# Feed-forward groups of 4, 6, 6, 6 units instead of 6, 4, 6, 6 in a macaron encoder layer on one core

## Chip, core and metric

One NeuronCore of a Trainium2 chip runs the whole kernel. The metric is the device time of one execution in microseconds, as the median of several runs of the kernel before and of the changed one on the same chip.

## What is computed

One layer of a streaming encoder for 576 tokens (512 of a prompt, 64 of a sample), width 1024, all in float32:

```
x = x + 0.5 * rmsnorm(swiglu_1(rmsnorm(x)))
x = x + rmsnorm(concat(retention, diff_attention)(rmsnorm(x) @ w_in) @ w_out)
x = x + 0.5 * rmsnorm(swiglu_2(rmsnorm(x)))
swiglu(h) = (silu(h @ wg) * (h @ wu)) @ wd        # 1024 -> 2816 -> 1024
```

The change touches the two feed-forward networks alone. It alters no value that is computed, only the order in which the hidden units are worked through.

## The kernel before

**Data.** Activations lie transposed (width on the 128 partitions, tokens along the free axis). The tokens are cut into two halves of 256 and 320 (`HN`) for the plain products, and into a front and a back of 288 (`HT`) for the seven-product ones. Every float32 operand is split into a rounded part `hi` and a rest `lo`, and each product is made as three matmuls, hi*hi, hi*lo and lo*hi. For weights `Weights.part` (L99) does this: a DMA on the SP queue brings 256 KB into a `raw` buffer (three of them, five more `raw2` for the seven-product blocks), ScalarE casts it to `whi` (L125), VectorE subtracts to get `wlo` (L126). Twelve such pairs can be held. `run` (L441) converts the weights six parts ahead of the chunk that it is about to issue.

**Feed-forward.** The hidden width 2816 is 22 units of 128. Units 0 to 3 (`PLAIN`) are made by plain gate/up chunks: `gate_up` (L604) multiplies for one token half (48 matmuls, L418 to L420), scales by the row's 1/rms (L612), applies silu on ScalarE (L613), multiplies (L614), and splits the result into an `a` tile (L185 on ScalarE, L186 on VectorE). Units 4 to 21 are made by `fast_unit` (L499), a seven-product scheme for a 2x2 block product: seven products P1 to P7 of 12 matmuls each (L513 to L515, 288 columns) in place of eight, with sums of weight blocks (`wsum`, L114 to L119) and sums of activation blocks (`tb`). Units are collected in groups (`GROUPS`); after a group its part of the down projection runs as four output chunks j for each token half (`down`, L627; the matmuls are L418 to L420 again, reading `a`). The first group's down chunks are copied from PSUM to `y` by ScalarE (L640), those of later groups are added to `y` by VectorE (L642).

**What has to happen before the first seven-product matmul.** The activations that the scheme reads must carry the 1/rms, which the plain chunks do without. `renorm` (L457) therefore scales the eight x rows (`scale`, L469), makes four sums and splits them into `tb` (`sums`, L480 with L185 and L186), and splits x again into `hhi` and `hlo` (`again`, L185 and L186). It is a generator of 18 steps; `ffn` hooks it behind the items of the order: it starts behind item 3, and items 3 to 7 (the last plain ones) advance it. The x tiles are read by it to its end; the `y` tiles of the down projection then take over the buffers of x (both are `big` tiles), and x is loaded again later (`reload_x`).

**Order.** A group's plain chunks come first, in the order c0, c1, c2 of half 0, the same of half 1, then c3 of half 0 and c3 of half 1 (`halves`, L428). In the kernel before, the first group has the four plain units and two seven-product ones, so its seven-product matmuls follow the last plain chunk at once. Each engine works through its own queue in the order given; the order on each engine is laid down by the tile scheduler when the program is built. PSUM is held in two double-bank tiles `pm` and four single banks (`pa`, `pb`, `A` and others); chunks take them in turn (`product`, L399). The seven products of a unit use a `pm` tile named `CB` and a bank `A`.

Of the kernel before, what the change touches and what calls it, by code (L numbers as in the profile page):

```python
# [23 lines left out]
HN = (256, 320)  # L24
DFF = 2816
MT = DFF // P
GROUPS = (6, 4, 6, 6)
PLAIN = 4
RENORM_STEPS = 4
HT = T // 2  # L30
BIG, IN_FFN = 16, 4
EPS = 1e-6
# [8 lines left out]
FIRST, LAST_FFN, LAST_MIX = 3, 4, 3  # L41
# [107 lines left out]
class Layer:  # L149
# [417 lines left out]
    def ffn_weights(self, f):  # L567

        io, w = self.io, self.w
        plan, m = [], 0  # L570
        for gi, nk in enumerate(GROUPS):
            units = list(range(m, m + nk))
# [8 lines left out]
    def ffn(self, f, h, pre_g, post_g, next_g):  # L581
# [4 lines left out]
        after, act, ys = [], {}, []  # L586
        first = [sum(GROUPS[:gi]) for gi in range(len(GROUPS))]
        with tc.tile_pool(name=f"ffn{f}", bufs=1) as fp:
# [12 lines left out]
            def a_tile():  # L601
                return fp.tile([P, 2, T], F32R, tag="a", name="a", bufs=max(GROUPS))

# [23 lines left out]
            def down(gi, j, parts_):  # L627
                def fn(half):
                    final = next_g is None and gi == len(GROUPS) - 1
                    s = slice(HOFF[half], HOFF[half] + HN[half])  # L630
                    parts = self.product(parts_, half, lambda kt: [act[first[gi] + kt][:, p, s] for p in range(2)], True,
                                         final and j == 3)
                    if gi == 0 and len(ys) == j:
                        ys.append(self.big("y"))
                    if gi == 0:
                        y[half][j] = self.cut(ys[j], half)
                    t = y[half][j]
                    for c, ps in parts:
                        if gi == 0:
                            nc.scalar.copy(t[:, c, :], ps)  # L640
                        else:
                            nc.vector.tensor_tensor(t[:, c, :], t[:, c, :], ps, ALU.add)  # L642
                    if gi == len(GROUPS) - 1:
                        self.sublayer_out(y, acc, half, j, post_g)
                        if j == 3 and final and half == 0:
                            self.finish_natural(y[0], acc[0], xn)
                        elif j == 3:
                            self.start_boundary(half, y, acc, next_g, after)
# [13 lines left out]
            n_plain = len(order)  # L662
            for kind, what, parts in plan:
                if kind == "plain":
                    continue
                if kind == "down":
                    later.append((parts, down(*what, parts)))
                    if what[1] == 3:
                        final = what[0] == len(GROUPS) - 1
                        order += self.halves(later, 4 if final else 1, 4 if final else 0, final and next_g is None)  # L670
# [7 lines left out]
            def step_renorm(n):  # L678
                for _ in range(n):
                    if renorm:  # L680
                        try:
                            next(renorm[0])
                        except StopIteration:
                            renorm.pop()
# [6 lines left out]
            def at(i, fn):  # L691
                old = hook.get(i)
                hook[i] = (lambda: (old(), fn())) if old else fn
            at(FIRST, start_renorm)
            for i in range(FIRST, n_plain - 1):
                at(i, lambda: step_renorm(RENORM_STEPS))
            at(n_plain - 2, lambda: step_renorm(1))
            at(n_plain - 1, lambda: step_renorm(1))
            last = max(i for i, o in enumerate(order) if o[2] is None)
            at(last, lambda: self.reload_x(self.spill if f else self.io["x"]))  # L700
            if next_g is None:
# [641 lines left out]
```

## Time and profile before

| | |
|---|---|
| median of 3 runs | 1173.41 us (1172.97 to 1173.81) |
| the profiled execution, its own time | 1175.34 us |
| its span in the trace | 1173.6 us |
| TensorE busy | 1137.6 us, 97% |
| VectorE busy | 830.9 us, 71% |
| ScalarE busy | 571.4 us, 49% |
| mean granted TensorE clock | 0.987 of full |

Busy time of TensorE is modelled from start to end of pipelined matmuls, so 97% does not say that it ran at its full pace. Where it waited or ran slowly is read from start times: the time between the first matmul of a stretch and the first of the next, against another stretch with the same matmuls.

### The profile page before, as it was taken

Reading aid. Unit: us, or ns where it says so; the run is one execution under the profiler, and the core shown is the slowest. Engines: PE = TensorE matmul, PEld = TensorE weight load, DVE = VectorE, ACT = ScalarE, POOL = GpSimd, SP = SyncE. Lnnn points to the kernel's source line nnn. Section 1 sums busy time; section 2 is a strip of 40 time slices with the busy share of each in tenths; the row PEclk is TensorE's granted clock in tenths of the full one; section 3 lists DMA queues with packets and bytes.
Section 4 is the critical chain, followed back from the end, with each engine's and each line's share of the span. In section 5 each row is a group of like instructions: output and inputs, shape, how many; then the busy total and the mean of one; then the engine's idle time right before and its main releaser. Section 6 shows DMA issues by size and latency. Waiting matters only on the chain.

```text
span 1173.6 us, 21248 instructions
## 1 busy us (share of the span) xinstructions
PE 1137.6 (97%) x8322; PEld 1114.4 (95%) x8322; DVE 830.9 (71%) x1634; ACT 571.4 (49%) x1102; POOL 43.6 (4%) x84
## 2 busy tenths in 40 slices
PE   8989999999999999999999999996999999999997
PEld 8989999999999999899999999996999999999997
DVE  7985586876586599869574574899547778658735
ACT  7664452552354564455432455665435346325543
POOL 0000000000000031020001010000000000000000
PEclk9989999999999999999999999998999999999998
DMA  7133241342235133242222222421414223313402
GB/s 259 46 92 102 64 136 45 100 130 68 64 90 197 55 94 119 67 125 82 66 83 61 72 85 74 139 68 47 134 54 118 72 83 110 107 50 96 164 25 81
DMA packets 57315, 109.20 MB, mean 93 GB/s; under 512 B 7008, under 2 KB 10336, under 8 KB 57216
## 3 DMA queue, kind: packets, MB, share of 16 engines
q1 hardware_dynamic: 51856, 91.97, 26.7%
q0 software_dynamic: 4352, 14.68, 3.7%
q8 instruction: 65, 1.06, 0.4%
q10 hardware_dynamic: 1008, 1.20, 0.3%
q14 instruction: 34, 0.28, 0.1%
HBM read 100.23 MB, written 7.60 MB: 92 GB/s over the span
## 4 chain that ended last, share of the span: by engine, by line
PE 82%; DVE 9%; DMA 4%; ACT 3%; issue 1%; SPq 0%; DVEq 0%; ACTq 0%
PE pm L418 9%; PE pm L419 9%; PE pm L420 9%; PE A L513 6%; PE A L514 6%; PE A L515 6%; PE CB L513 5%; PE CB L515 4%; PE CB L514 4%; PE pb L418 2%; PE pa L418 2%; PE pb L420 2%; PE pa L419 2%; PE pa L420 2%; PE pb L419 2%; DVE wlo L126 2%
## 5 line engine op out<-in xcount | busy, mean ns | idle before, releaser
L125 ACT CAST whi<-raw 128x512 fp32r<-128x512 f32 x336 | 206.4, 619 | 242.0 <-PE pm L419 84.5
L126 DVE TENSOR_TENSOR wlo<-raw,whi 128x512 fp32r<-128x512 f32 x336 | 229.4, 688 | 113.6 <-ACT whi L125 109.3
L418 PE MATMUL pm<-hhi,whi 128*128 128x320 f32 (+1 forms) x496 | 152.0, 307 | 1.2 <-ACT hhi L253 1.2
L420 PE MATMUL pm<-hhi,wlo 128*128 128x320 f32 (+1 forms) x496 | 147.9, 299 | 0.4 <-DVE wlo L126 0.2
L419 PE MATMUL pm<-hlo,whi 128*128 128x320 f32 (+1 forms) x496 | 147.7, 298 | 0.3 <-DVE hlo L254 0.3
L420 PE MATMUL pm<-a,wlo 128*128 128x320 f32 (+1 forms) x448 | 133.0, 297 | 0.0
L419 PE MATMUL pm<-a,whi 128*128 128x320 f32 (+1 forms) x448 | 133.0, 297 | 0.0
L418 PE MATMUL pm<-a,whi 128*128 128x320 f32 (+1 forms) x448 | 132.7, 296 | 0.0
L513 PE MATMUL A<-tb,whi 128*128 128x288 f32 x432 | 129.7, 300 | 0.0
L514 PE MATMUL A<-tb,whi 128*128 128x288 f32 x432 | 128.5, 297 | 0.0
L515 PE MATMUL A<-tb,wlo 128*128 128x288 f32 x432 | 127.9, 296 | 0.0
L125 ACT CAST whi<-wsum 128x512 fp32r<-128x512 f32 x108 | 67.0, 621 | 84.3 <-PE pm L419 28.2
L513 PE MATMUL CB<-hhi,whi 128*128 128x288 f32 x288 | 86.6, 301 | 15.7 <-ACT e L529 8.8
L126 DVE TENSOR_TENSOR wlo<-wsum,whi 128x512 fp32r<-128x512 f32 x108 | 74.5, 690 | 34.5 <-ACT whi L125 33.0
L418 PEld LDWEIGHTS pm<-hhi,whi 128*128 128x128 f32 x496 | 94.1, 190 | 2.2 <-ACT hhi L253 1.5
L419 PEld LDWEIGHTS pm<-hlo,whi 128*128 128x128 f32 x496 | 94.1, 190 | 1.1 <-DVE hlo L254 0.5
L420 PEld LDWEIGHTS pm<-hhi,wlo 128*128 128x128 f32 x496 | 93.9, 189 | 1.0 <-DVE wlo L126 0.8
L515 PE MATMUL CB<-hhi,wlo 128*128 128x288 f32 x288 | 85.8, 298 | 0.0
L514 PE MATMUL CB<-hlo,whi 128*128 128x288 f32 x288 | 85.6, 297 | 0.0
L419 PEld LDWEIGHTS pm<-a,whi 128*128 128x128 f32 x448 | 85.0, 190 | 0.3 <-DVE a L186 0.3
L420 PEld LDWEIGHTS pm<-a,wlo 128*128 128x128 f32 x448 | 85.0, 190 | 0.0
L418 PEld LDWEIGHTS pm<-a,whi 128*128 128x128 f32 x448 | 84.9, 190 | 0.0
(333 smaller groups left out, 2926.2 us busy)
## 6 DMA issues: line engine op xcount, KB each, us to landing
raw<-in_w0gs SPq DMA_DIRECT2D x72, 256.0 KB, 2.7
raw<-in_w1gs SPq DMA_DIRECT2D x72, 256.0 KB, 2.7
raw<-in_win SPq DMA_DIRECT2D x56, 256.0 KB, 3.1
raw<-in_w0d SPq DMA_DIRECT2D x44, 256.0 KB, 2.7
raw<-in_w1d SPq DMA_DIRECT2D x44, 256.0 KB, 2.8
raw<-in_w0gu SPq DMA_DIRECT2D x16, 256.0 KB, 5.8
raw<-in_wout SPq DMA_DIRECT2D x16, 256.0 KB, 2.9
raw<-in_w1gu SPq DMA_DIRECT2D x16, 256.0 KB, 3.3
```

What stands on the lines that cost most here:

```text
L125: nc.scalar.copy(hi, raw)
L126: nc.vector.tensor_tensor(lo, raw, hi.bitcast(F32), ALU.subtract)
L418: nc.tensor.matmul(outs[c], lhsT=hi[:, k, cs], rhs=rh, start=kt == 0, stop=False)
L419: nc.tensor.matmul(outs[c], lhsT=hi[:, k, cs], rhs=rl, start=False, stop=False)
L420: nc.tensor.matmul(outs[c], lhsT=lo[:, k, cs], rhs=rh, start=False, stop=kt == len(kts) - 1)
L513: nc.tensor.matmul(out, lhsT=hi[:, k, :], rhs=rh, start=first and k == 0, stop=False, skip_group_check=True)
L514: nc.tensor.matmul(out, lhsT=hi[:, k, :], rhs=rl, start=False, stop=False, skip_group_check=True)
L515: nc.tensor.matmul(out, lhsT=lo[:, k, :], rhs=rh, start=False, stop=last and k == 3, skip_group_check=True)
```

## The change

`GROUPS` becomes (4, 6, 6, 6). The first group is then the four plain units alone. Its eight down half chunks (24 matmuls each, L418 to L420) stand between the last plain gate/up chunk and the first seven-product matmul; the 18 seven-product units follow as three groups of six. The number of matmuls, of weight parts and of down chunks is the same. `renorm` is advanced by three steps behind each of items 3 to 7 and is finished behind item 7 (before: four steps, then single ones, ended behind item 7 as well).

```diff
-GROUPS = (6, 4, 6, 6)
+GROUPS = (4, 6, 6, 6)
-RENORM_STEPS = 4
+RENORM_STEPS = 3
...
-            for i in range(FIRST, n_plain - 1):
+            for i in range(FIRST, n_plain):
                 at(i, lambda: step_renorm(RENORM_STEPS))
-            at(n_plain - 2, lambda: step_renorm(1))
-            at(n_plain - 1, lambda: step_renorm(1))
+            at(n_plain - 1, lambda: step_renorm(100))
```

TensorE, second feed-forward, end of the plain chunks: before (numbers behind a name are the scheduler's tile numbers).

```order
L418 MATMUL pm_9418<-hhi_8764,whi_8989 128x320
L419 MATMUL pm_9418<-hlo_8765,whi_8989 128x320
L420 MATMUL pm_9418<-hhi_8764,wlo_8990 128x320
L513 MATMUL CB_9490<-tb_9164,whi_9001 128x288
L514 MATMUL CB_9490<-tb_9165,whi_9001 128x288
L515 MATMUL CB_9490<-tb_9164,wlo_9002 128x288
```

The same place now:

```order
L418 MATMUL pm_9389<-hhi_8764,whi_8989 128x320
L419 MATMUL pm_9389<-hlo_8765,whi_8989 128x320
L420 MATMUL pm_9389<-hhi_8764,wlo_8990 128x320
L418 MATMUL pm_9488<-a_8898,whi_8995 128x256
L419 MATMUL pm_9488<-a_8898,whi_8995 128x256
L420 MATMUL pm_9488<-a_8898,wlo_8996 128x256
```

What follows the last plain chunk reads the `a` tiles of the plain units and no longer the `tb` of `renorm`.

VectorE, second feed-forward, around L612 of the last plain chunk (unit 3, half 1): before.

```order
L480 TENSOR_TENSOR sums_9172<-x3_4456,sums_9172 128x576
L186 TENSOR_TENSOR tb_9171<-sums_9172,tb_9170 128x576
L186 TENSOR_TENSOR hlo_8571<-x0_4453,hhi_8570 128x2x256
L186 TENSOR_TENSOR tb_9171<-sums_9172,tb_9170 128x576
L186 TENSOR_TENSOR hlo_8637<-x1_4454,hhi_8636 128x2x256
L186 TENSOR_TENSOR hlo_8701<-x2_4455,hhi_8700 128x2x256
L186 TENSOR_TENSOR hlo_8765<-x3_4456,hhi_8764 128x2x256
L612 TENSOR_TENSOR gu_9467<-pm_9418,r_pre_9150 128x640
L186 TENSOR_TENSOR hlo_8571<-x0_4453,hhi_8570 128x2x32
```

The same place now:

```order
L186 TENSOR_TENSOR tb_9163<-sums_9168,tb_9162 128x576
L480 TENSOR_TENSOR sums_9168<-x3_4456,sums_9168 128x576
L612 TENSOR_TENSOR gu_9438<-pm_9389,r_pre_9146 128x640
L186 TENSOR_TENSOR tb_9165<-x0_4453,tb_9164 128x576
L186 TENSOR_TENSOR tb_9163<-sums_9168,tb_9162 128x576
L614 TENSOR_TENSOR gu_9438<-gu_9438 128x320
L480 TENSOR_TENSOR x1_4454<-x3_4456,x1_4454 128x2x288
L186 TENSOR_TENSOR a_9377<-gu_9438,a_9377 128x320
L480 TENSOR_TENSOR sums_9168<-x2_4455,sums_9168 128x576
```

L612, L614 and the split into `a` of the last plain chunk now stand ahead of the last sums, of five splits into `tb` and of all splits into `hlo`.

ScalarE, second feed-forward, where the copies into `y` begin (in brackets what a row waits for; DMASW are the POOL queue's DMAs): now. Before, these copies stood behind the two seven-product units, and the first of them had no wait for VectorE.

```order
L185 CAST a_9377<-gu_9438 128x320 [waits DVE_49]
L185 CAST tb_9164<-x1_4454 128x576 [waits DVE_49]
L185 CAST tb_9166<-sums_9168 128x576 [waits DVE_49] x2
L640 COPY y_9513<-pm_9488 128x2x256 [waits DMASW2_49,DVE_49,DMASW6_49,PE_49,Activation_49]
L640 COPY y_9513<-pa_9515 128x320 [waits PE_49]
L640 COPY y_9513<-pb_9516 128x320 [waits PE_49]
L640 COPY y_9584<-pm_9559 128x2x256 [waits DMASW3_49,DVE_49,DMASW7_49,PE_49,Activation_49]
L640 COPY y_9650<-pa_9624 128x256 [waits DMASW0_49,DMASW4_49,DVE_49,PE_49]
L640 COPY y_9584<-pm_9586 128x2x320 [waits PE_49]
```

The first copy of each output chunk now waits for VectorE, since its `y` tile takes the buffer of an x tile that `renorm` still reads. The matmul that needs the first of these copies (its `pm` tile is the one that the copy empties) stands on TensorE here:

```order
L420 MATMUL pb_9625<-a_9058,wlo_9319 128x256
L418 MATMUL pa_9624<-a_9377,whi_9318 128x256
L419 MATMUL pa_9624<-a_9377,whi_9318 128x256
L420 MATMUL pa_9624<-a_9377,wlo_9319 128x256
L418 MATMUL pm_9586<-a_8898,whi_9300 128x320 [waits Activation_49]
```

Ahead of it stand three half chunks (`pm_9488`, `pa_9515` with `pb_9516`, `pm_9559`) and 21 of the 24 matmuls of a fourth (`pa_9624` with `pb_9625`).

## Rows read from the trace of the kernel before

**Rows 1.** The page, part 1: engine, busy us, share of the span, instructions.

```profile
PE 1137.6 (97%) x8322; PEld 1114.4 (95%) x8322; DVE 830.9 (71%) x1634; ACT 571.4 (49%) x1102; POOL 43.6 (4%) x84
```

**Rows 2.** Waits of TensorE, whole span: total us, times, longest us.

```profile
PE CB L513 <- ACT e L529: 8.8, 2, 7.1
PE CB L513 <- DVE g L537: 6.9, 4, 2.4
PE CB L513 <- DVE gu L612: 6.0, 2, 3.1
```

**Rows 3.** Timeline, TensorE, first feed-forward: start us, us, engine line op.

```profile
62.63 0.29 PE L513 MATMUL CB<-tb,whi 128*128 128x288 f32 x1
...
92.75 0.28 PE L418 MATMUL pa<-a,whi 128*128 128x256 f32 x1
92.87 0.28 PE L419 MATMUL pa<-a,whi 128*128 128x256 f32 x1
...
131.15 0.29 PE L513 MATMUL CB<-tb,whi 128*128 128x288 f32 x1
...
176.03 0.28 PE L418 MATMUL pm<-a,whi 128*128 128x256 f32 x1
...
201.80 0.29 PE L513 MATMUL CB<-tb,whi 128*128 128x288 f32 x1
...
268.93 0.28 PE L418 MATMUL pm<-a,whi 128*128 128x256 f32 x1
```

**Rows 4.** Timeline, TensorE, second feed-forward, the first two groups.

```profile
795.33 0.29 PE L513 MATMUL CB<-tb,whi 128*128 128x288 f32 x1
...
834.15 0.28 PE L418 MATMUL pm<-a,whi 128*128 128x256 f32 x1
...
872.54 0.29 PE L513 MATMUL CB<-tb,whi 128*128 128x288 f32 x1
...
917.89 0.28 PE L418 MATMUL pm<-a,whi 128*128 128x256 f32 x1
```

**Rows 5.** Windows: us, busy PE, PEld, DVE, ACT, POOL, PEclk, DMA share, GB/s.

```profile
201.80:268.90 67.10, 67.10 (x506) 66.91 (x505) 54.74 (x95) 38.89 (x71) 0.00 (x0) 1.00 0.39 112
795.30:809.50 14.20, 4.27 (x24) 3.72 (x23) 14.18 (x28) 6.55 (x14) 0.00 (x0) 0.75 0.00 0
369.00:376.00 7.00, 4.57 (x34) 4.31 (x33) 5.91 (x12) 4.65 (x9) 0.00 (x0) 1.00 0.60 159
1113.00:1120.00 7.00, 4.57 (x23) 4.34 (x23) 5.22 (x11) 3.93 (x7) 0.00 (x0) 0.76 0.53 150
```

**Rows 6.** Timeline, VectorE, the end of `renorm` in both feed-forwards, and four weight splits.

```profile
68.95 0.81 DVE L612 TENSOR_TENSOR gu<-pm,r_pre 128x640 f32<-128x640 f32 x1
69.69 1.29 DVE L186 TENSOR_TENSOR hlo<-x,hhi 128x64 fp32r<-128x64 f32 x5
...
802.60 0.75 DVE L480 TENSOR_TENSOR sums<-x,sums 128x576 f32<-128x576 f32 x1
803.26 0.75 DVE L186 TENSOR_TENSOR tb<-sums,tb 128x576 fp32r<-128x576 f32 x1
...
807.01 0.82 DVE L612 TENSOR_TENSOR gu<-pm,r_pre 128x640 f32<-128x640 f32 x1
807.74 1.29 DVE L186 TENSOR_TENSOR hlo<-x,hhi 128x64 fp32r<-128x64 f32 x5
...
817.50 2.49 DVE L126 TENSOR_TENSOR wlo<-raw,whi 128x512 fp32r<-128x512 f32 x4
```

**Rows 7.** Tile `y`: the copies of L640 on ScalarE, ns min/median/max.

```profile
L640 ACT COPY y<-pm x10: 582/636/697, 102.5 to 867.5; 128x640 f32<-128x640 f32 x5, 128x512 f32<-128x512 f32 x5
```

**Rows 8.** Timeline, TensorE, the last group of the second feed-forward, start and end.

```profile
1049.18 0.29 PE L513 MATMUL CB<-tb,whi 128*128 128x288 f32 x1
...
1120.76 0.31 PE L418 MATMUL pm<-a,whi 128*128 128x320 f32 x1
```

## Prediction

> **What bounds the kernel now.** The page comes first: TensorE is busy for 97% of the span and VectorE for 71% [rows 1]. So only two things can make the kernel faster: less work for TensorE, or the places where it stands still or runs slowly. The change takes no matmul away, so I look for such places. The list of TensorE's waits has three large lines, all at L513, the start of a product of the seven-product scheme [rows 2]: 8.8 us for the copy `e`, 6.0 us for `gu` of a plain chunk, 6.9 us for `g`. Their sum is 21.7 us.
>
> The timeline tells where they lie and what they cost with the slow clock that goes with them. A group of six units far from any disturbance takes 268.93 - 201.80 = 67.13 us, which is 11.19 per unit [rows 3], and in that stretch the clock is granted in full [rows 5]. The two units of the first group take 92.75 - 62.63 = 30.12 us in the first feed-forward [rows 3] and 834.15 - 795.33 = 38.82 in the second [rows 4], where 22.38 would do. The group of four takes 176.03 - 131.15 = 44.88 and 917.89 - 872.54 = 45.35, where 44.75 would do. So the loss sits behind the last plain chunk, and VectorE shows why: from 795.30 to 809.50 it is busy for 14.18 of 14.20 us while TensorE gets 4.27 us of work, at 0.75 of the clock [rows 5]. VectorE is finishing `renorm`, and L612 of the last plain chunk, whose PSUM tile TensorE wants back, stands behind it at 807.01 [rows 6].
>
> **The change, term by term.**
>
> *First: the two units move.* In each feed-forward the groups of two and four become one group of six between a down block of 192 matmuls and one of 288. These are just the neighbours of the old third group, so I give it that group's 67.13 us. First feed-forward: 30.12 + 44.88 - 67.13 = 7.87 us saved. Second: 38.82 + 45.35 - 67.13 = 17.04. Together 24.9. The down blocks keep their matmuls and change places, at no cost as long as nothing in them waits; that is the next question.
>
> *Second: do the down chunks that now follow the plain ones wait for their input?* They read `a` of the four plain units; the last to come is unit 3, half 1. A pair of half chunks of this block takes (201.80 - 176.03) / 4 = 6.44 us; 256 columns take 0.12 per matmul, 2.88 per half chunk [rows 3], which leaves 3.56 for the 320 columns, 0.148 each. The second half chunk needs that `a` for its last quarter: 2.88 + 18 x 0.148 = 5.5 us after the start of the block, at 68.2 and 800.9.
>
> When VectorE has it I count on its order, with 0.62 us for a weight split or any other operation of 128x512 (2.49 / 4) and 0.67 for one of 128x576 (802.60 to 803.26) [rows 6]. Second feed-forward: ahead of this L612 four weight operations fewer stand (6 against 10, 2.5 us), eight operations on 576 elements fewer (three sums, five splits into `tb`: 5.4) and four splits into `hlo` fewer (2.5). So L612 comes at 807.01 - 10.4 = 796.6, later than the end of its product, near 795.6 (795.33 and the length of one matmul). Then follow L612 (0.74), two splits into `tb`, L614 (0.4), one sum and the split into `a` (0.49): 3.6 us, ready at 800.2. It is wanted at 800.9, so the margin is 0.7. First feed-forward: four weight operations, two splits into `tb` and four into `hlo` fewer put L612 at 68.95 - 6.3 = 62.7, the moment its product ends; `a` is ready near 66, wanted at 68.2.
>
> *Third: a new wait.* The copies into `y` (L640) now wait for VectorE, as the `y` tile takes the buffer of an x tile which `renorm` still reads. The x tile of chunk 0 is free after the first of the small `hlo` splits: 807.74 in the second feed-forward before [rows 6], now 2.5 earlier for the weight operations and 0.8 later for L614 and the `a` split that have moved ahead of it: 806.0, and 0.2 for itself. The copy takes some 0.6 [rows 7], so the `pm` tile is free at 806.9. TensorE wants it after three half chunks and 21 matmuls: 795.33 + 6.44 + 45 x 0.12 = 807.2. The margin is 0.3. In the first feed-forward the same sum gives free at 68.8 and wanted, by a later chunk, after two pairs, at 75.5: hidden with 6.7 us to spare. Behind the waiting copy on ScalarE stand the casts of the first seven-product weights; they are wanted when the block ends, at 795.33 + 25.8 = 821, so 14 us cover them.
>
> The two margins of the second feed-forward are thin. From below a wait costs nothing. From above it can cost what the old order would give, `hlo` at 807.74 + 0.8 and a copy, 2.0 us after the point at which the tile is wanted; one wait of 2.4 us with the slow clock behind it is the worst that the last group shows, 4.4. I take 0.5 us, near the lower end, since both counts come out on the free side.
>
> *Nothing else.* `RENORM_STEPS` and the single steps move VectorE's work within items 3 to 7, and that is in the counts above. The SP queue brings the same 256 KB parts in the new order; the eight parts of the first down block come while the plain chunks run, where DMA share is 0.00 from 795.30 to 809.50 [rows 5]. VectorE's load in a steady group is 54.74 of 67.10 us [rows 5], so the longer first group is not bound by it. The POOL queue issues nothing new.
>
> **Sum.** 24.9 - 0.5 = 24.4 us. The profiled execution took 1175.34 us, of them 1173.6 span; it would take 1150.9, with a span of 1149.2. The median of the runs is 1.93 us below that execution, so the median goes from 1173.41 to 1149.0.
>
> **Rivals.**
>
> *The copy comes late and the clock falls.* If VectorE reaches the end of `renorm` two microseconds later than counted, TensorE stops for about 2.4 us in the second feed-forward's first down block. Two stops of 2.43 us at L513 stand in the trace: at 369 to 376 the granted clock stays at 1.00, at 1113 to 1120 it falls to 0.76 [rows 5], so a stop of this length can cost either. The stretch with the fall takes 1120.76 - 1049.18 = 71.58 us [rows 8], 4.4 over 67.13. The time would be 1148.5 + 4.4 = 1152.9. The Trainium skill (TensorE: Matmul & The Clock Gate, A second HAM failure mode: psum-queue depth-cycling) has a rule against this change: short idle moments between groups of matmuls, while PSUM banks are handed on, can make the clock swing between its two levels. By that rule the bank handed on late would bring the slow clock along and 1152.9 is the time; the trace agrees in one of the two stops.
>
> *The new first group of six ends like the last one.* In the last group of each feed-forward the last unit waits 2.4 us for `g` [rows 2], because VectorE's queue is held by a weight split whose DMA is late. If the new first six-unit group did the same in both feed-forwards, once with the fall of the clock, it costs 2.4 + 4.4 = 6.8: 1155.8. Against it: the old third group has the same neighbours and shows none of it.
>
> *The loss only moves.* If the down block ends before `renorm` is through, the first product waits again. But that product now comes 25.8 us after the last plain one, and `renorm` was through some 15 us after it (795.33 to 810 [rows 4, 6]), with more work for VectorE ahead of it. It would need 10 us more for the first microsecond of a wait, and 24 us of new waits for a time near 1173.
>
> *Slower.* The longer first group runs short of weights: while the block of small half chunks (24 matmuls for two weight parts, not three) runs, TensorE uses up the twelve held pairs faster than three `raw` buffers refill them, and each of the 12 units then waits. That decides from 24.4 / 12 = 2.0 us per unit, 13.2 in place of 11.19; at 2.5 the time is 1179. Against it: the old third group follows a block of the same size at 11.19 per unit.
>
> **Chances.** Forecast 0.62, late copy 0.17, end of the first six 0.14, loss moves 0.04, slower 0.03. The range 1147.0 to 1154.0 holds the forecast, its bounds (no wait, 1148.5; half of a last-group wait less, 1147) and the late copy, 0.79. A measurement here tells apart about 0.2%, 2.3 us. All cases but the last two are faster by more: faster 0.94, same 0.03, slower 0.03.
>
> **What would show it.** In the profile after: no stop over 1 us at L513 behind the plain chunks; the first seven-product matmul 25.8 us after the last plain one in both feed-forwards; three groups of six, the first two near 67.1 us; 17 us saved in the second feed-forward and 8 in the first; the granted clock full there. In the list of waits `e` and `gu` are gone and `g` keeps its two of 2.4. I am wrong if TensorE waits for ScalarE at L418 in the down block by more than 1 us (third term), for `a` (second term), or if the first six units take over 68 us (first term).

## The result and the profile after

The changed kernel took 1152.13 us (median of four runs, 1150.70 to 1153.00), the kernel before beside it 1173.19 (four runs, 1172.39 to 1173.81). The ratio is 0.982 with a 95% interval of 0.9803 to 0.9837: 21.1 us less. The forecast was 24.4 us less and 1149.0, with a range of 1147.0 to 1154.0.

The page of the changed kernel, part 1, as in [rows 1]:

```profile
PE 1129.9 (98%) x8322; PEld 1109.2 (97%) x8322; DVE 833.8 (73%) x1634; ACT 573.2 (50%) x1102; POOL 43.0 (4%) x84
```

The instruction counts of the four compute engines are those of before. The list of TensorE's waits, in the columns of [rows 2]:

```profile
PE CB L513 <- DVE g L537: 4.8, 2, 2.4
PE ssq_pre L223 <- DVE sq_pre L220: 2.2, 2, 1.7
PE pm L418 <- ACT hhi L253: 1.4, 1, 1.4
```

The lines for `e` and `gu` at L513 are gone, 14.8 us of waits. Of `g` two waits are left, the two of 2.4 us in the last groups. The timeline of TensorE, the first matmul of each stretch; it answers to [rows 3, 4]:

```profile
62.31 0.28 PE L418 MATMUL pa<-a,whi 128*128 128x256 f32 x1
...
87.91 0.29 PE L513 MATMUL CB<-tb,whi 128*128 128x288 f32 x1
...
155.04 0.28 PE L418 MATMUL pm<-a,whi 128*128 128x256 f32 x1
...
193.44 0.29 PE L513 MATMUL CB<-tb,whi 128*128 128x288 f32 x1
...
260.63 0.28 PE L418 MATMUL pm<-a,whi 128*128 128x256 f32 x1
...
787.50 0.28 PE L418 MATMUL pm<-a,whi 128*128 128x256 f32 x1
...
813.12 0.29 PE L513 MATMUL CB<-tb,whi 128*128 128x288 f32 x1
...
880.26 0.28 PE L418 MATMUL pm<-a,whi 128*128 128x256 f32 x1
...
918.66 0.29 PE L513 MATMUL CB<-tb,whi 128*128 128x288 f32 x1
...
985.85 0.28 PE L418 MATMUL pa<-a,whi 128*128 128x256 f32 x1
```

Read the differences. The new first down block takes 87.91 - 62.31 = 25.60 us in the first feed-forward and 813.12 - 787.50 = 25.62 in the second. The first group of six then takes 155.04 - 87.91 = 67.13 and 880.26 - 813.12 = 67.14, the second 67.19 in both. The windows show the same stretches of the second feed-forward at the full clock (2.4 GHz), and below them the last group of each feed-forward, which the change did not touch; columns as in [rows 5]:

```profile
787.50:813.12 25.62, 25.62 (x195) 25.62 (x193) 23.67 (x42) 14.47 (x29) 0.00 (x0) 1.00 0.17 51
813.12:880.26 67.14, 67.14 (x506) 66.95 (x505) 55.51 (x96) 39.55 (x73) 0.00 (x0) 1.00 0.41 121
...
299.03:369.10 70.07, 67.63 (x507) 66.99 (x505) 53.77 (x93) 38.79 (x71) 2.24 (x4) 1.00 0.40 126
1024.24:1095.95 71.71, 69.23 (x506) 68.53 (x505) 53.99 (x93) 38.68 (x71) 2.16 (x4) 0.98 0.39 122
```

So the mechanism is the forecast one. Two questions were left for experiments. Is the saving made of the three terms, feed-forward by feed-forward, and are the thin margins real? And why do the spans of the two profiled executions lie 1173.6 - 1148.5 = 25.1 us apart, while the medians lie 21.1 apart?

### The profile page after: what moved, and what is told of

Its sections match the earlier page's. It is cut to its first block, busy times and chain, and to the rows that moved or that the text cites. A ratio compares the mean times of both kernels' runs of the same rounds, so it can differ in the third digit from the quotient of the medians.

```text
span 1148.5 us, 21267 instructions
## 1 busy us (share of the span) xinstructions
PE 1129.9 (98%) x8322; PEld 1109.2 (97%) x8322; DVE 833.8 (73%) x1634; ACT 573.2 (50%) x1102; POOL 43.0 (4%) x84
## 4 chain that ended last, share of the span: by engine, by line
PE 89%; DVE 5%; DMA 3%; ACT 1%; issue 1%; SPq 0%; DVEq 0%; ACTq 0%
PE pm L418 10%; PE pm L419 10%; PE pm L420 10%; PE A L513 7%; PE A L515 7%; PE A L514 7%; PE CB L513 5%; PE CB L515 5%; PE CB L514 5%; PE pb L418 2%; PE pa L418 2%; PE pa L419 2%; PE pb L420 2%; PE pb L419 2%; PE pa L420 2%; DMA raw<-in_win 2%
## 5 line engine op out<-in xcount | busy, mean ns | idle before, releaser
L418 PE MATMUL pm<-hhi,whi 128*128 128x320 f32 (+1 forms) x496 | 152.7, 308 | 1.4 <-ACT hhi L253 1.4
L420 PE MATMUL pm<-hhi,wlo 128*128 128x320 f32 (+1 forms) x496 | 148.2, 299 | 0.0
L420 PE MATMUL pm<-a,wlo 128*128 128x320 f32 (+1 forms) x452 | 134.1, 297 | 0.0
L418 PE MATMUL pm<-a,whi 128*128 128x320 f32 (+1 forms) x452 | 134.0, 296 | 0.0
L513 PE MATMUL A<-tb,whi 128*128 128x288 f32 x432 | 128.9, 298 | 0.1
L418 PEld LDWEIGHTS pm<-hhi,whi 128*128 128x128 f32 x496 | 94.7, 191 | 2.3 <-ACT hhi L253 1.7
L420 PEld LDWEIGHTS pm<-hhi,wlo 128*128 128x128 f32 x496 | 94.7, 191 | 0.2
L513 PE MATMUL CB<-hhi,whi 128*128 128x288 f32 x288 | 85.4, 297 | 4.8 <-DVE g L537 4.8
L418 PEld LDWEIGHTS pm<-a,whi 128*128 128x128 f32 x452 | 85.8, 190 | 0.0
L420 PEld LDWEIGHTS pm<-a,wlo 128*128 128x128 f32 x452 | 85.8, 190 | 0.0
```

What stands on the lines that cost most here:

```text
L418: nc.tensor.matmul(outs[c], lhsT=hi[:, k, cs], rhs=rh, start=kt == 0, stop=False)
L420: nc.tensor.matmul(outs[c], lhsT=lo[:, k, cs], rhs=rh, start=False, stop=kt == len(kts) - 1)
L513: nc.tensor.matmul(out, lhsT=hi[:, k, :], rhs=rh, start=first and k == 0, stop=False, skip_group_check=True)
```

## The experiments

The theory was the prediction's: two seven-product units behind the plain chunks wait for `renorm`, and a down block in their place covers it. Rivals: the stepping of `renorm` alone does it; fewer and larger groups do it; the gain comes from one place alone.

| kernel | median us | before beside it | difference | ratio, 95% interval |
|---|---|---|---|---|
| the change, second time | 1152.49 | 1175.21 | -22.7 | 0.981 (0.9783 to 0.9836) |
| the change, third time | 1151.16 | 1173.76 | -22.6 | 0.9811 (0.9791 to 0.9831) |
| first feed-forward alone | 1165.88 | 1175.21 | -9.3 | 0.9924 (0.99 to 0.9947) |
| second feed-forward alone | 1159.75 | 1175.21 | -15.5 | 0.9876 (0.985 to 0.9903) |
| new groups, old stepping | 1153.81 | 1175.21 | -21.4 | 0.9821 (0.9793 to 0.985) |
| old groups, new stepping | 1170.52 | 1173.76 | -3.2 | 0.9974 (0.9961 to 0.9987) |
| five groups | 1157.08 | 1173.64 | -16.6 | 0.9859 (0.9835 to 0.9883) |
| four more operations | 1156.63 | 1173.76 | -17.1 | 0.9855 (0.9833 to 0.9878) |
| eight more operations | 1154.94 | 1173.64 | -18.7 | 0.984 (0.9817 to 0.9864) |
| the change, late reload | 1143.16 | 1173.76 | -30.6 | 0.9743 (0.9723 to 0.9764) |
| before, late reload | 1164.78 | 1173.64 | -8.9 | 0.993 (0.9904 to 0.9957) |
| before, second time | 1175.04 | 1173.50 | +1.5 | 1.0012 (1.0002 to 1.0022) |

The last row is the yardstick: the same kernel beside itself differs by 1.5 us in the median, so a difference of that size says nothing here.

### The change again

> The changed kernel once more, unchanged, beside the kernel before, five rounds. Its profiled execution had a span of 1148.5 us and the kernel before's one of 1173.6, 25.1 apart, while the medians lie 21.1 apart. Theory A (the kernel before's profiled execution had more slow clock behind the plain chunks than its median run): the median of before stays near 1173, the changed kernel near 1151 to 1152, and the changed kernel's second feed-forward has again no stop over 1 us at its first down block. Theory B (the margin of 0.1 us at the first y copy is lost in most executions): a profile with a stop over 0.5 us at L418 in the first down block of the second feed-forward, the granted clock at half behind it, and a span of 1150 to 1151 in place of 1148.5.

Measured: 1152.49 us, profiled span 1148.7. No stop over 0.5 us in the first down block of the second feed-forward, which took 813.39 - 787.46 = 25.93 us; group of six 67.14. Theory B's stop and half clock are not there. A third time it ran beside a later group of kernels:

> The changed kernel unchanged, as the yardstick for the kernels beside it: 1151 to 1153 us. In its last groups two stops of 2.7 us at L513; each has been followed by half clock in some executions (group 71.6 us) and not in others (70.0), so two profiles of it may differ by 1.7 us for each of the two.

Measured: 1151.16 us, span 1147.9. Here the third term shows itself as a line of the list of TensorE's waits:

```profile
PE pm L418 <- ACT y L640: 0.2, 1, 0.2
```

The block took 814.09 - 788.02 = 26.07 us, 0.47 over the first feed-forward's 25.60. The last groups took 71.45 and 70.14 us.

### One feed-forward at a time

`GROUPS` is made a pair, one tuple for each feed-forward, and used as `GROUPS[f]`; the old stepping stays with the old groups.

```diff
-GROUPS = (4, 6, 6, 6)
+GROUPS = ((4, 6, 6, 6), (6, 4, 6, 6))
...
-        for gi, nk in enumerate(GROUPS):
+        for gi, nk in enumerate(GROUPS[f]):
```

> Groups 4, 6, 6, 6 and the new stepping in the first feed-forward alone. Theory: each feed-forward gains its own part, by the profile 7.9 us here (30.12 + 44.88 - 67.13), so near 1165.3 us, with a second feed-forward like that of the kernel before (38.8 us for the first two seven-product units). If the whole shortfall of the median gain (3.3 us) belonged to the first feed-forward, it would gain 4.6: 1168.6. Rival, the gain comes from one place alone, the second feed-forward: 1173.

> Groups 4, 6, 6, 6 and the new stepping in the second feed-forward alone. Theory: 17.0 us less by the profile (38.82 + 45.35 - 67.13), 1156.2; 13 to 14 less, 1159 to 1160, if the median execution of the kernel before had less slow clock there than the profiled one or if the thin margin of the first y copy is lost at the median. The first feed-forward shows 30.1 us for its first two seven-product units as before. The two one-sided kernels together give the gain of the change (21.1) within 1.5 us; if they do not, the feed-forwards affect one another.

Measured: 9.3 us less and 15.5 less, together 24.8, against 22.7 for the whole change beside the same runs of the kernel before. Both feed-forwards take part. The expectation wanted the sum within 1.5 us of 21.1; it is 3.7 above that, and 2.1 above the whole change beside it. Each of the three gains is known only to some 3 us (the intervals in the table), and the moved stretches are nearly as long as in the whole change (25.60 and 67.14 us in the first kernel, 26.14 and 67.14 in the second), so no effect of one feed-forward on the other is shown. The first of these kernels still has the old second feed-forward, so its trace shows this one a second time. Timeline of TensorE, the first two units and the group of four:

```profile
791.29 0.29 PE L513 MATMUL CB<-tb,whi 128*128 128x288 f32 x1
...
827.37 0.28 PE L418 MATMUL pm<-a,whi 128*128 128x256 f32 x1
...
865.76 0.29 PE L513 MATMUL CB<-tb,whi 128*128 128x288 f32 x1
...
910.64 0.28 PE L418 MATMUL pm<-a,whi 128*128 128x256 f32 x1
```

The two units take 36.08 us and the group of four 44.88, where [rows 4] gave 38.82 and 45.35. That is 3.2 us less to be saved.

### The kernel before again

> The kernel before once more, unchanged, for a second profile of it. The forecast took 38.82 us for the first two seven-product units of the second feed-forward and 45.35 for the group of four from one profile; the one-sided kernel with the old second feed-forward showed 36.08 and 44.88. Theory (the profiled execution had a chance stop of 2.16 us at 827.17, for a late weight DMA, which the usual execution has not): 36.1 and 44.9 us here, no stop over 1 us in the last products of the two units, list of waits with g twice and not four times, so that the first term is 7.7 + 13.8 = 21.5 and not 24.9. Rival (the stop belongs to the kernel before and the one-sided kernels shifted it): near 38.8 again.

Measured: 1175.04 us beside 1173.50; the profiled execution took 1171.56. The timeline of TensorE, first the start of the two units, then the two stops at their end and the next down block:

```profile
795.01 0.29 PE L513 MATMUL CB<-tb,whi 128*128 128x288 f32 x1
...
827.61 0.40 PE L513 MATMUL CB<-hhi,whi 128*128 128x288 f32 x1 [0.44 <-DVE g L537]
...
830.29 0.40 PE L513 MATMUL A<-tb,whi 128*128 128x288 f32 x1 [0.82 <-DVE f L540]
831.98 0.28 PE L418 MATMUL pm<-a,whi 128*128 128x256 f32 x1
```

The two units take 36.97 us, the group of four 44.88. The stop at their end is there, but small. In the profile that the forecast was made from it is longer. The rows are of ScalarE and of TensorE:

```profile
826.89 0.62 ACT L125 CAST whi<-raw 128x512 fp32r<-128x512 f32 x1 [2.44 <-DMA raw<-in_w1d]
...
829.33 0.40 PE L513 MATMUL CB<-hhi,whi 128*128 128x288 f32 x1 [1.86 <-DVE g L537]
```

A weight DMA landed late, the cast waited 2.44 us for it, VectorE's split stood behind the cast and the addition into `g` behind the split, so TensorE waited. Behind this stop the granted clock fell to half:

```profile
829.79:833.20 3.41, 3.41 (x16) 3.41 (x15) 2.11 (x5) 0.76 (x2) 0.00 (x0) 0.50 0.67 213
```

In the second profile of the kernel before it is full from 812.50 us to the end of the two units. By an estimate, 3.41 us at half the clock are 1.7 us lost, about as much as the stop itself. Four traces with the same code in this stretch give 38.82, 36.08, 36.04 (the kernel before with late reload, below) and 36.97. The waits at the end of the two units differ from one execution to the next, from 0.2 to 1.9 us, and the forecast took the largest, with its half clock, for the usual one. Why the DMA landed later in that execution was not found. The expectation of 36.1 held within 0.9, and no wait there is over 1 us; `g` stands in the list three times, not twice.

### The stepping of renorm

New groups with the old stepping:

```diff
-RENORM_STEPS = 3
+RENORM_STEPS = 4
...
-            for i in range(FIRST, n_plain):
+            for i in range(FIRST, n_plain - 1):
                 at(i, lambda: step_renorm(RENORM_STEPS))
-            at(n_plain - 1, lambda: step_renorm(100))
+            at(n_plain - 2, lambda: step_renorm(1))
+            at(n_plain - 1, lambda: step_renorm(1))
```

> Groups 4, 6, 6, 6 with renorm advanced as before: four steps behind each of items 3 to 5, then one and one. The splits into hlo now stand ahead of L612 of the last plain chunk on VectorE again, as do three sums and five splits into tb (5.4 + 2.5 = 7.9 us of work). Theory (the second term, a of the last plain chunk has a margin of 0.5 us in the second feed-forward): the a tile comes near 800.5 - 793.0 = 7.5 us late, so TensorE stops 6 to 8 us at L418 in the first down block of the second feed-forward, with slow clock behind it: 7 to 11 us above the changed kernel, 1159 to 1163; in the first feed-forward 0 to 3 us more. Rival, only the groups count and the stepping is an adornment: within 1.5 us of the changed kernel.

Measured: 1153.81 us, 1.3 above the change, where 7 to 11 were expected. The premise, a late `a`, held. VectorE has `a` of the last plain chunk only here, behind the `hlo` splits:

```profile
798.96 0.82 DVE L612 TENSOR_TENSOR gu<-pm,r_pre 128x640 f32<-128x640 f32 x1
...
801.98 0.49 DVE L186 TENSOR_TENSOR a<-gu,a 128x320 fp32r<-128x320 f32 x1
```

The down block began at 788.92, so the second half chunk would have wanted `a` at 794.45 and stood still for 8 us. TensorE did not stand still, and its timeline shows why:

```profile
790.96 0.28 PE L420 MATMUL pm<-a,wlo 128*128 128x256 f32 x1
791.08 0.31 PE L418 MATMUL pa<-a,whi 128*128 128x320 f32 x1
...
792.80 0.38 PE L418 MATMUL pm<-a,whi 128*128 128x256 f32 x1 [0.68 <-ACT a L185]
...
799.84 0.39 PE L418 MATMUL pm<-a,whi 128*128 128x256 f32 x1 [1.42 <-DVE gu L612]
```

After 18 of the 24 matmuls of the first half chunk, the second (`pa`, 320 columns) begins, the first is finished in between, and the last quarter of the 320 columns stands behind two more half chunks of 256, nearly whole. The order of TensorE's matmuls changed with that of VectorE, since the scheduler lays down both; so what is left are two short stops, 0.68 us for the `a` of half 0 and 1.42 us for the PSUM tile that the late L612 empties, and the whole block takes 817.19 - 788.92 = 28.27 us, 2.7 over the change. The rival ("within 1.5 us") had the number, but the stops are real. That the median shows less than 2.7 us lies within the yardstick; in this profile, unlike the change's, the clock also stayed full in both last groups (70.12 and 70.07 us).

Old groups with the new stepping, the kernel before with the other three lines of the diff:

> The kernel before with the new stepping of renorm alone, groups 6, 4, 6, 6. VectorE has L612 of the last plain chunk earlier by four hlo splits, three sums and three tb splits, but the seven-product units still stand right behind the plain chunks and need all of tb and the split x. Theory (the place of the two units is what costs): 0 to 3 us below the kernel before. Rival (the stepping alone held L612 back, and the groups do little): 15 us or more below it.

Measured: 3.2 us less, just past the expected 0 to 3. L612 comes earlier, but TensorE now waits for the split x itself:

```profile
PE A L514 <- DVE hlo L186: 11.9, 2, 7.5
```

So the groups bring the gain and the stepping is a detail of it.

### Five groups

```diff
-GROUPS = (4, 6, 6, 6)
+GROUPS = (4, 2, 4, 6, 6)
```

> Groups 4, 2, 4, 6, 6 with the new stepping: the four plain units alone are the first group, as in the change, but the two and the four seven-product units stay separate groups with a down block of 96 and of 192 matmuls. Theory (what costs is that two seven-product units stand right behind the plain chunks, not the number of groups): 22.4 us for the two units and 44.9 for the four, the change's time plus 0.2 us for the down blocks and up to 3 for eight more additions on VectorE: 1151 to 1155. Rival (it is the larger group of six that saves, by fewer ends of a group): 1160 or more.

Measured: 1157.08 us, between the theory's range and the rival's. The timeline of TensorE in the first feed-forward decides for the theory:

```profile
87.98 0.29 PE L513 MATMUL CB<-tb,whi 128*128 128x288 f32 x1
...
110.51 0.28 PE L418 MATMUL pm<-a,whi 128*128 128x256 f32 x1
...
123.35 0.29 PE L513 MATMUL CB<-tb,whi 128*128 128x288 f32 x1
...
168.17 0.28 PE L418 MATMUL pm<-a,whi 128*128 128x256 f32 x1
...
193.94 0.29 PE L513 MATMUL CB<-tb,whi 128*128 128x288 f32 x1
```

The two units take 22.53 us behind a down block, the four 44.82; with their down blocks it is 193.94 - 87.98 = 105.96, against 193.44 - 87.91 = 105.53 in the change. The second feed-forward is the same (22.52 and 44.83). The rest of the 5 us lies outside of what was moved: the stretch from the in-projection's start to the out-projection's took 267.33 us in place of 263.8 in the change's second profile, and the second feed-forward's plain chunks 57.67 in place of 54.69. In these plain chunks TensorE waits 2.88 us for VectorE (1.57 in the change's second profile), and the granted clock is at 0.51 around it:

```profile
747.15 1.22 PE L223 MATMUL ssq_pre<-sq_pre,ones 128*128 128x256 f32 x2 [2.88 <-DVE sq_pre L220]
```

```profile
746.90:750.40 3.50, 3.25 (x10) 2.68 (x11) 1.31 (x4) 1.00 (x2) 0.00 (x0) 0.51 0.24 75
```

The change with late reload, below, also has half clock in these chunks (56.65 us), so this part is not tied to the five groups. What lengthens the mixer was not pursued.

### The margin of the first y copy

More work for VectorE at the end of `renorm`, on a scratch tile:

```diff
+        for _ in range(4):
+            nc.vector.tensor_tensor(made[0], made[0], made[1], ALU.add)
         for pair in range(2):
             again(pair, slice(0, HN[0]))
```

> The change, and four more VectorE operations on 128x576 (0.67 us each, 2.7 in all, on a scratch tile whose content is no longer needed) among the large hlo splits at the end of renorm in both feed-forwards, ahead of the split that gives the x tile of the first y copy free. TensorE's order is the same. Theory (the third term: margin near 0.1 us in the second feed-forward, over 6 in the first): TensorE stops 2.5 us at L418 for the copy L640 in the second feed-forward and not at all in the first: 2.5 us above the changed kernel if the clock stays, 4.2 if it falls for 3.4 us. Rival, the margin was over 2.7 us: no stop, same time. Rival, VectorE is short of time in the whole block: stops in both, 5 us or more.

Measured: 1156.63 us, 5.5 above the change beside it, somewhat more than either figure. TensorE's list of waits has the forecast line (L642 is the copy, two lines lower in this kernel):

```profile
PE pm L418 <- ACT y L642: 2.1, 1, 2.1
```

The windows up to the end of the stop, behind it, and to the end of the block:

```profile
789.34:804.00 14.66, 12.60 (x100) 12.40 (x99) 14.66 (x28) 6.11 (x13) 0.00 (x0) 1.00 0.00 0
804.20:807.60 3.40, 3.40 (x15) 3.40 (x14) 3.40 (x7) 1.16 (x4) 0.00 (x0) 0.50 0.23 81
807.60:818.78 11.18, 11.18 (x82) 11.18 (x81) 7.70 (x13) 6.49 (x12) 0.00 (x0) 1.00 0.32 80
```

The clock fell to half (1.2 GHz) right behind the stop; the block took 29.45 us, 3.85 over 25.60, and the six units behind it 67.99 in place of 67.14, with a wait of 0.6 us for `g`. No stop in the first feed-forward (25.60). This is the prediction's first rival, forced: the Trainium skill (TensorE: Matmul & The Clock Gate, A second HAM failure mode: psum-queue depth-cycling) tells of a kernel in which TensorE idles for short moments between groups of matmuls, often, while it cycles through PSUM banks, and the clock swings. The trace agrees in part: here one such stop, of 2.1 us, was followed by half clock. So 2.7 us of work cost a stop of 2.3 us between two matmuls: the margin is a few tenths. In five profiles with the new second feed-forward and the new stepping the block takes 25.62, 25.93, 26.07, 26.14 and 25.99 us, 0.35 over 25.60 in the mean, and in none of them does the clock fall there.

With eight operations:

> The change with eight more VectorE operations of 0.67 us (5.4 us) at the end of renorm in both feed-forwards, in place of four. TensorE's order is the same. Second feed-forward: a stop of 5.0 us at L418 for the copy L640 (2.34 with four operations, 2.7 more). First feed-forward: by the prediction's margin of 6.7 us no stop; by a new count from the trace with four operations, where pa was given free at 72.04 us and taken at 72.05, the margin was 2.7 and a stop of 2.7 us now stands there. Time: near 1162 by the new count with half clock behind both stops, near 1159 by the prediction's margin.

Measured: 1154.94 us, no worse than four, where 1159 to 1162 and a stop of 5.0 us were expected. On VectorE the operations alternate with the `hlo` splits, and only four of the eight came ahead of the split that frees the first tile; the stop is again 2.1 us, the block 29.43. As a dose it failed. It corrects my new count of the first feed-forward, though: the first copy came at 72.00 us there, and the next `pa` pair was taken at 71.72 without a stop, so that pair is another one. The prediction's 6.7 us were not contradicted, and were not tested to their end.

### The stop that is left: x loaded later

The last group of each feed-forward takes 70.07 and 71.71 us in the change's profile, 2.9 and 4.5 over the 67.19 of the group ahead of it; before the change it was much the same ([rows 8] for the second). POOL loads x again there, after which the weights come late:

```profile
349.82 2.24 POOL L265 DMA_DIRECT2D x<-in_x  x4 [349.36 <-PE A L515]
```

The edit holds the DMAs back until the last unit's `a` exists:

```diff
         for j, t in enumerate(tiles):
+            self.nc.gpsimd.tensor_copy(t[:, 0, 0:1], late[:, 0, 0:1].bitcast(F32))
             self.nc.gpsimd.dma_start(out=t, in_=src[:, 2 * j:2 * j + 2, :])
...
-            at(last, lambda: self.reload_x(self.spill if f else self.io["x"]))
+            at(last, lambda: self.reload_x(self.spill if f else self.io["x"], act[MT - 1]))
             if next_g is None:
-                at(last + 1, natural_x)
+                at(last + 3, natural_x)
```

> The change, and x is loaded again only when the a tile of the last unit exists (a copy of one column by POOL into each x tile ahead of its DMA, and the transposes of x two items later). Theory (the last unit of each feed-forward waits for weights because four DMAs of x take the bandwidth at 349.8 and 1075.0 us): the stops of 2.7 us at 363 and 1088 go, both last groups take 67.2 us in place of 70.1 and 71.7, no half clock after them: 6 to 7.5 us less than the changed kernel, 1144.5 to 1146. Rival, the wait belongs to the end of the product scheme itself (no next unit, so the last products have no cover): the stops stay and the time is within 1 us of the changed kernel, or above it if x then comes late for the boundary or for the transposes.

Measured: 1143.16 us, 8.0 below the change beside it and 30.6 below the kernel before. The windows of the two last groups, which answer to the last two rows of the change's windows:

```profile
300.14:367.33 67.19, 67.18 (x506) 66.94 (x505) 54.15 (x93) 38.92 (x71) 0.00 (x0) 1.00 0.32 96
1024.21:1091.41 67.20, 67.19 (x507) 66.95 (x506) 54.25 (x93) 38.95 (x71) 0.00 (x0) 1.00 0.32 95
```

Both are at the undisturbed length, and `g` is gone from the list of waits. The theory holds; its range (6 to 7.5) was half a microsecond short. The same edit in the kernel before:

> The kernel before with x loaded late, as in the version of the change that beat it by 8.0 us. Theory (the last group's stop has its own cause, apart from the change): both last groups take 67.2 us, 7 to 8 us below the kernel before, 1165.5 to 1167, while the two first units still take 30 and 34 to 39 us. Rival (the two gains are one, both from how the last units meet the weights in the new order): under 3 us.

Measured: 8.9 us less, a little past the 7 to 8 expected, both last groups 67.2 us, the first two units 30.32 and 36.04. It is a gain of its own, beside that of the change.

## Why the prediction was right, and by how much it was off

**First term, mechanism right, size off in the second feed-forward.** The group of six came out at the 67.13 us that the old third group had lent. In the first feed-forward four traces give 30.1 us in the mean for the old two units (30.12, 29.43, 30.32, 30.34), so 7.8 us were saved, as forecast. In the second the step "38.82 + 45.35 - 67.13 = 17.04" is the one that failed: 38.82 holds a stop of 1.86 us for a weight DMA that landed late in that execution, with 3.41 us of half clock behind it, and 45.35 a wait of 0.2 us for `g` that the others lack. The three other traces give 36.04 to 36.97 and about 44.88: 13.8 to 14.7 us. The hint stood in [rows 2]: `g` had four waits of 6.9 us in all, two of them the known 2.4; the other two, 1.86 and 0.20, were taken into the sum as if they belonged to the place.

**Second term, right.** `a` of the last plain chunk came 0.5 us ahead of its use (792.5, wanted at 793.0), forecast 0.7. The rows of the change, VectorE and TensorE:

```profile
792.04 0.48 DVE L186 TENSOR_TENSOR a<-gu,a 128x320 fp32r<-128x320 f32 x1
```

```profile
793.02 0.31 PE L418 MATMUL pa<-a,whi 128*128 128x320 f32 x1
```

The price of a late `a` was not a full stop where it was tried: with the old stepping the scheduler laid other matmuls ahead, and the block lost 2.7 us instead of 8.

**Third term, right in mechanism.** Forecast 0.5 us, measured 0 to 0.5. The 0.5 was chosen between two bounds and not counted, so its nearness is partly luck. The rows of the change, VectorE, then ScalarE, then TensorE:

```profile
796.39 3.77 DVE L186 TENSOR_TENSOR hlo<-x,hhi 128x512 fp32r<-128x512 f32 x9
```

```profile
798.57 0.59 ACT L640 COPY y<-pm 128x512 f32<-128x512 f32 x1 [3.33 <-DVE hlo L186]
```

```profile
799.30 0.33 PE L418 MATMUL pm<-a,whi 128*128 128x320 f32 x1
```

The copy ends at 799.16, and TensorE takes the tile at 799.30: 0.1 us to spare where 0.3 was worked out. In the four other unforced profiles the copy is late, and TensorE waits 0.1 to 0.2 us for it.

**Sum.** 7.8 + 13.8 to 14.7 - 0.35 gives 21.3 to 22.2 us; measured were 21.1, 22.7 and 22.6. From the profiled execution that the forecast started from to that of the change it came out almost exactly: 24.4 us forecast, 25.1 between the spans. The spans lie further apart than the medians because the profiled execution of before was a long one for its kernel (1175.34 against a median of 1173.41) and that of the change a short one (1150.70 against 1152.13). One part of the first is now known, the stop with the half clock behind it; the rest is within what the same kernel differs by from run to run, which for the kernel before was 1170.08 to 1176.76 in fifteen runs.

**Rivals.** By the time alone, 1152.1 is nearer to the late copy's 1152.9 than to the forecast of 1149.0, and the range held it because it reached up to that rival; so far the hit is luck, and only the traces tell the two apart. A copy that is late by 2 us, with half clock behind it, is in none of the five unforced profiles, and when forced it costs 3.85 us in the block, near the 4.4 taken. The first six do not end like the last one: 67.13 and 67.14. The loss does not move: no wait at L513 behind the plain chunks. The longer group is not short of weights: 67.14 / 6 = 11.19 us per unit. In the chances, the three faster cases add up to 0.93, not to the 0.94 that stands there.

## What to carry to other kernels

Where an engine at its limit stands behind another that prepares the next kind of work, put a block whose inputs are ready in between; its length is the cover, and a stretch with the same neighbours elsewhere in the trace is the best price list for the result. Before a stretch from one profile goes into a sum, divide its waits, and the half clock behind them, into those that repeat and those that do not, by a second stretch or a second profile. A bulk load that is issued as soon as its buffer is free can delay the small loads that the engines are waiting for; if it is not needed soon, tie it to a later event.

## What the runs showed that was not expected

A stop of the same length does not always bring the slow clock. In twelve profiles with the early reload TensorE's 2.7 us gap in the last groups occurs 24 times; 15 of them are followed by half clock (the group then takes 71.4 to 72.1 us), 9 are not (69.9 to 70.4). By these lengths the fall itself costs about 1.5 us. A forecast that adds it to each stop is too high by as much in 9 cases of 24.

Between 350 and 360 us, where the four DMAs of x run, the DMA engines were busy for 89% of their time at 333 GB/s, and a weight cast on ScalarE waited 4.27 us for its DMA; with the load deferred the same ten microseconds show 45% and 134 GB/s:

```profile
350.00:360.00 10.00, 10.00 (x78) 10.00 (x77) 4.48 (x8) 3.19 (x7) 2.05 (x4) 1.00 0.89 333
```

```profile
350.00:360.00 10.00, 10.00 (x77) 10.00 (x76) 6.72 (x12) 5.74 (x11) 0.00 (x0) 1.00 0.45 134
```

(The first window is of the change, the second of the change with late reload.)
